# Two channel-major projections in seven products: the output gate and the gMLP gate of a hybrid trunk

## The chip, the cores and the metric

The kernel runs on one core of one Trainium2 chip. A core has five engines that each work through their own instructions in order: TensorE (PE, matrix products; PEld is its weight load), VectorE (DVE), ScalarE (ACT), GpSimd (POOL) and SyncE (SP, which issues the DMAs). The metric is the device time of one execution in microseconds; lower is better. Before the change it is 828.49 us, the median of 3 runs (826.92 to 829.87).

## The reference

One layer over 512 frames of 1024 channels, in float32. After an RMSNorm, one input projection of 7168 columns gives eight pieces: `zu, zv` (512 each), `zq, zf, zi, zo, g_a, g_b` (1024 each).

```
h = rmsnorm(x, norm_mix);  proj = h @ w_in
u = gelu(zu); v = layernorm(gelu(zv))
y_a = (u * (W_s v + b)) @ w_up_a            # gMLP: W_s mixes frames inside blocks of 128
f = sigmoid(zf), k = sigmoid(-zf), q = silu(zq), values = zi
o = recurrence(q, k, values, log f)          # HGRN2, 8 heads of 128
o = rmsnorm(o, norm_g) * silu(zo)            # the output gate
y_b = o @ w_up_b
mix = sigmoid(g_a) * y_a + sigmoid(g_b) * y_b
x = x + mix @ w_out
x = x + square(relu(rmsnorm(x) @ w_ff1)) @ w_ff2;  out = rmsnorm(x)
```

## The kernel before

**Arithmetic.** Each float32 operand is split into a high part H and a rest L (`split`, L95: H by ScalarE, L = x - H by VectorE), and a product is three matmuls, H times H, H times L, L times H (`mm3`, L113). Weights come as 512 KB tiles `raw` on SyncE's queue into 4 buffers (`wraw`, L89), in the order of `_plan`; their split (`operand`, L99) goes into 5 buffers `WH`/`WL`.

**Three forms of the input projection.** `chan_proj` (L314): 128 channels on the partitions, 512 frames wide, 8 blocks of k, so 24 matmuls of 512 columns. `tok_proj` (L332): frames on the partitions, 256 channels wide, 96 matmuls of 256 columns. `seven` (L124): 256 channels on the partitions by 512 frames as a 2x2 block product in seven block products instead of eight; each is 4 blocks of k in three matmuls, so 84 matmuls of 256 columns. It needs four sums of weight halves (`s1` to `s4`, L148 to L156) that are split as well, and frame operands `n1` to `n4` that are made once by `frames_operands` (L174). One product goes into an `acc` bank `x`, others into a pair of banks `zy`, of which there is one set in the first half of the kernel; `x` is read out in between.

**Order in the program around the change.** Normalised frames `hT`; `zv` by `tok_proj`; LayerNorm of `v` on VectorE and `frames_operands`; four groups of the gMLP branch, each with `chan_proj` for `zu` (L378), the block mixing `pm` and the product `y`; the values of round 0 (`values(0)`, L399); the upward projection `upa` into `part0`. Then four rounds of two heads. A round has `gates_round` (F and Q by `seven`), `hgrn_pair` (the recurrence: a chain of doublings on VectorE, small `sp` matmuls on TensorE, then `outputs` into `o_n` with frames on the partitions), the values of the next round and, from round 1 on, `gate_o` of the round before: `zo` by `tok_proj`, SiLU, product with `o_n`. Then gate A (four `seven`, L572), gate B (four `seven`, L576) with the last `gate_o` in the midst, and `onto_channels` (L583): eight heads of `o_n` are transposed (`py`), scaled by the norm's gain and split into `ybH`, `ybL`, which `upb` (L604) multiplies. The output projection and the MLP follow and are not touched.

**What sets the order.** The code's order is the priority; a scheduler then interleaves the instructions of each engine ahead of time, so that one `seven` is woven into another or into a round. On the chip each engine works in that fixed order and waits where an operand or a buffer is late. Tiles of a pool that is closed are handed on, tile by tile, once their last reader is done.

Of the kernel before, what the change touches and what calls it, by code (L numbers as in the profile page):

```python
# [48 lines left out]
def _plan():  # L49

    names = []
    for g in range(2):
        names += [("tok", ZV + 256 * g, k) for k in (0, 1)]
    names += [("chan", ZU + 128 * g) for g in range(4)]
    names += [("tok", ZI, k) for k in (0, 1)]
    names += [("upa", d) for d in range(4)]
    for r in range(4):
        names += [("tok", ZI + 256 * r, k) for k in (0, 1) if r]
        names += [("chan", z + 128 * h) for z in (ZF, ZQ) for h in (2 * r, 2 * r + 1)]
        names += [("tok", ZO + 256 * r, k) for k in (0, 1)]  # L60
    names += [("chan", GA + 128 * d) for d in range(8)]
# [12 lines left out]
def trunk_kernel(ctx: ExitStack, tc: tile.TileContext, A: dict, out: bass.AP):  # L74
# [156 lines left out]
    def rstd_of_halves(pool, ms, tag):  # L231

        e = pool.tile([P, 1], F32, tag=f"re_{tag}", bufs=2, name=f"re_{tag}")
        nc.gpsimd.tensor_scalar(e, ms[:, 0:1], EPS, None, ALU.add)
        return rstd_of(pool, ms[:, 1:2], 1, e, tag)
# [125 lines left out]
    px_stack.close()  # L361
    for t in range(NT):
# [13 lines left out]
    yaL = pya.tile([P, NG, S], F32R, name="yaL")  # L376
    for g in range(NG):
# [12 lines left out]
    def values(r):  # L390
        V = held("V", r).rearrange("p a b -> p (a b)").rearrange("p (t c) -> p t c", t=NT)

        def evac_v(tp, acc):
            nc.scalar.copy(V[:, 2 * tp:2 * tp + 2, :], acc)

        tok_proj(ZI + 256 * r, evac_v)
        return V

    V = values(0)  # L399


# [10 lines left out]
    left3 = ExitStack()  # L412
    pt = left3.enter_context(tc.tile_pool(name="pt", bufs=1, side="left", reuse_waits="tile"))
    left2 = ExitStack()
    hg = left2.enter_context(tc.tile_pool(name="hg", bufs=1, side="left", reuse_waits="tile"))
    ps_sc = left3.enter_context(tc.tile_pool(name="ps_sc", bufs=1, space=bass.MemoryType.PSUM))
# [10 lines left out]


    def gates_round(r, V):
# [6 lines left out]
        def fin_q(i, cols, src):  # L436
            qc = Q[:, i, cols]
            sig = pt.tile([P, S], F32, tag="sig", bufs=2, name="sig")[:, cols]
            nc.scalar.activation(sig, src, AF.Sigmoid, scale=-1.0 if i else 1.0)
            nc.vector.scalar_tensor_tensor(qc, src, -1.0 if i else 1.0, sig, ALU.mult, ALU.mult)  # L440
# [106 lines left out]
    def gate_a(d):  # L547
        g = pt.tile([P, 2, S], F32, tag="ga", bufs=1, name="ga")
# [47 lines left out]
    yb = [onto_channels(pyb, h) for h in range(4)]  # L596
    right2.close()
# [299 lines left out]
```

## Time and profile before

| what | value |
|---|---|
| median of the runs | 828.49 us |
| the profiled execution's own time | 830.5 us |
| its span, first to last instruction | 828.4 us |
| PE busy | 809.9 us, 98% |
| DVE busy | 597.6 us, 72% |
| ACT busy | 429.7 us, 52% |
| PE's clock, mean granted | 0.994 of full speed |

The busy time of an engine is the time in which at least one of its instructions is shown as running. Matmuls overlap: each is shown from its issue to the end of its result, so the time that one costs in a stream is the distance from its start to the next one's start, and not its shown duration. VectorE's instructions overlap a little at their ends in the same way.

### The profile page before, as it was taken

How to read it: one execution, taken by the hardware profiler on the slowest of the kernel's cores; microseconds unless marked ns; L12 is line 12 of the kernel's file. 1: busy time of each engine (PE TensorE's matmuls, PEld its weight loads, DVE VectorE, ACT ScalarE, POOL GpSimd, SP SyncE). 2: the span in 40 equal slices, each digit the busy share in tenths (PEclk: the TensorE clock that was granted, in tenths of full speed). 3: DMA queues.
4: the chain of work that ended last, by engine and by line, in shares of the span. 5: the costliest groups of instructions: out<-in, count | busy, mean ns of one | idle time of the engine just before them, and what ended most of it. 6: DMA issues, size and time to landing. Idle time of an engine off the chain costs nothing.

```text
span 828.4 us, 16602 instructions
## 1 busy us (share of the span) xinstructions
PE 809.9 (98%) x7026; PEld 740.8 (89%) x7026; DVE 597.6 (72%) x797; ACT 429.7 (52%) x720; POOL 49.4 (6%) x80
## 2 busy tenths in 40 slices
PE   8999999999999999999899999999999999999996
PEld 7989899998999999999778889999999988778884
DVE  6686257856767788865474369887777575899896
ACT  5543363637536446654432343767767542555464
POOL 2010000000000100100000022000000000010103
PEclk9999999999999999999999999999999999999998
DMA  8242232302313113332335411333333396193802
GB/s 315 73 143 64 63 105 79 104 28 81 99 53 103 52 54 102 102 103 81 123 102 168 162 56 48 97 109 102 103 104 118 117 296 176 40 283 93 239 10 102
DMA packets 27212, 92.29 MB, mean 111 GB/s; under 512 B 4161, under 2 KB 4161, under 8 KB 27138
## 3 DMA queue, kind: packets, MB, share of 16 engines
q1 hardware_dynamic: 24834, 83.89, 31.6%
q0 software_dynamic: 1728, 6.29, 4.2%
q8 instruction: 55, 0.90, 0.5%
q10 hardware_dynamic: 576, 1.05, 0.3%
q14 instruction: 19, 0.16, 0.1%
HBM read 89.13 MB, written 2.10 MB: 110 GB/s over the span
## 4 chain that ended last, share of the span: by engine, by line
PE 93%; ACT 2%; DVE 2%; DMA 1%; issue 1%; POOL 0%; SPq 0%; POOLq 0%; ACTq 0%; DVEq 0%
PE acc L120 12%; PE acc L121 11%; PE acc L122 11%; PE prodx L120 7%; PE prodx L121 7%; PE prodx L122 7%; PE prodzy L120 5%; PE prodzy L122 5%; PE prodzy L121 5%; PE hm L121 3%; PE hm L120 3%; PE hm L122 3%; PE sp L456 2%; PE y L122 2%; PE y L120 2%; PE y L121 2%
## 5 line engine op out<-in xcount | busy, mean ns | idle before, releaser
L97 DVE TENSOR_TENSOR WL<-raw,WH 128x1024 fp32r<-128x1024 f32 (+1 forms) x134 | 146.8, 1101 | 79.8 <-ACT WH L96 79.0
L96 ACT ACTIVATE WH<-raw 128x1024 fp32r<-128x1024 f32 (+1 forms) x134 | 128.7, 963 | 137.8 <-PE acc L121 27.2
L97 DVE TENSOR_TENSOR WL<-s,WH 128x1024 fp32r<-128x1024 f32 x60 | 73.3, 1222 | 39.7 <-ACT WH L96 38.9
L120 PE MATMUL acc<-WH,hTH 128*128 128x256 f32 x320 | 92.5, 289 | 1.3 <-ACT F L434 1.3
L121 PE MATMUL acc<-WL,hTH 128*128 128x256 f32 x320 | 91.4, 286 | 0.0
L122 PE MATMUL acc<-WH,hTL 128*128 128x256 f32 x320 | 91.0, 285 | 0.0
L96 ACT ACTIVATE WH<-s 128x1024 fp32r<-128x1024 f32 x60 | 63.7, 1062 | 39.0 <-PE prodx L121 15.7
L120 PEld LDWEIGHTS acc<-WH,hTH 128*128 128x128 f32 x320 | 60.9, 190 | 1.8 <-ACT F L434 1.6
L121 PEld LDWEIGHTS acc<-WL,hTH 128*128 128x128 f32 x320 | 61.0, 191 | 0.1
L122 PEld LDWEIGHTS acc<-WH,hTL 128*128 128x128 f32 x320 | 60.9, 190 | 0.0
L121 PE MATMUL hm<-WL,aH 128*128 128x512 f32 x96 | 38.1, 396 | 0.0
L122 PE MATMUL hm<-WH,aL 128*128 128x512 f32 x96 | 38.0, 395 | 0.0
L120 PE MATMUL hm<-WH,aH 128*128 128x512 f32 x96 | 37.9, 396 | 0.0
L120 PE MATMUL prodzy<-hTH,WH 128*128 128x256 f32 x128 | 36.2, 283 | 0.0
L122 PE MATMUL prodzy<-hTH,WL 128*128 128x256 f32 x128 | 36.0, 282 | 0.0
L121 PE MATMUL prodzy<-hTL,WH 128*128 128x256 f32 x128 | 36.0, 281 | 0.0
L120 PE MATMUL prodx<-n2H,WH 128*128 128x256 f32 x120 | 34.0, 283 | 0.7 <-ACT u L147 0.7
L96 ACT ACTIVATE WH<-rawx 128x1024 fp32r<-128x1024 f32 x24 | 25.1, 1054 | 18.5 <-issue 10.7
L120 PE MATMUL prodzy<-n1H,WH 128*128 128x256 f32 x120 | 33.8, 282 | 0.0
L120 PE MATMUL prodx<-n4H,WH 128*128 128x256 f32 x120 | 33.8, 282 | 0.0
L121 PE MATMUL prodx<-n4L,WH 128*128 128x256 f32 x120 | 33.8, 281 | 0.0
L122 PE MATMUL prodzy<-n1H,WL 128*128 128x256 f32 x120 | 33.6, 280 | 0.0
(313 smaller groups left out, 2494.3 us busy)
## 6 DMA issues: line engine op xcount, KB each, us to landing
raw<-in_w_dram SPq DMA_DIRECT2D x128, 512.0 KB, 3.7
rawx<-in_w_dram SPq DMA_DIRECT2D x18, 512.0 KB, 8.6
rawx<-in_w_dram POOLq DMA_DIRECT2D x6, 512.0 KB, 7.2
raw<-in_w_dram POOLq DMA_DIRECT2D x6, 512.0 KB, 8.5
part<-in_x_dram SPq DMA_DIRECT2D x4, 512.0 KB, 6.1
x<-in_x_dram SPq DMA_DIRECT2D x4, 512.0 KB, 6.5
out_dram<-x ACTq DMA_DIRECT2D x4, 256.0 KB, 2.7
out_dram<-x SPq DMA_DIRECT2D x4, 256.0 KB, 2.3
```

What stands on the lines that cost most here:

```text
L96: nc.scalar.activation(H, src, AF.Copy)
L97: nc.vector.tensor_tensor(L, src, H.bitcast(F32), ALU.subtract)
L120: nc.tensor.matmul(acc, ah, bh, start=first and i == 0, stop=False, **kw)
L121: nc.tensor.matmul(acc, ah, bl, start=False, stop=False, **kw)
L122: nc.tensor.matmul(acc, al, bh, start=False, stop=last and i == n - 1, **kw)
L456: nc.tensor.matmul(sp[p * C:(p + 1) * C, (h * NT + t) * n:(h * NT + t + 1) * n], K[:, h, c0:c0 + C], x(h, c0), start=True, stop=True)
```

## The change

The output gate `zo` is made with channels on the partitions by `seven` (four calls, one for two heads each), into tiles that earlier rounds held; SiLU is applied there. Its place is after the four rounds; gate A's four calls take the place in the rounds that `gate_o` had. `onto_channels` now multiplies the transposed, scaled head with the gate and splits the product, and its first four heads stand ahead of gate B in the code. `zu` is made by `seven` as well, in two calls. The values of rounds 0 and 1 are made before and after the gMLP groups. `rstd_of_halves` only gets other arguments.

```
-    names += [("tok", ZI, k) for k in (0, 1)]
+    names += [("tok", ZI + 256, k) for k in (0, 1)]
...
+    V = [values(0)]
     for g in range(NG):
-        zu = chan_proj(ZU + 128 * g)
-        u = gp.tile([P, S], F32, tag="u", bufs=2, name="u")
-        nc.scalar.activation(u, zu, AF.Gelu)
+        if g % 2 == 0:
+            u2 = pya.tile([P, 2, S], F32, tag="ug", bufs=1, name="ug")
+            seven(("chan", ZU + 128 * g), ("chan", ZU + 128 * g + 128), rhs, pya, ps_sc, u2, act_by_sign(u2, AF.Gelu), True)
+        u = u2[:, g % 2, :]
...
-    V = values(0)
+    V.append(values(1))
...
+    def silu(g, i, cols, src):
+        sig = hg.tile([P, S], F32, tag="sig", bufs=2, name="sig")[:, cols]
+        nc.scalar.activation(sig, src, AF.Sigmoid, scale=-1.0 if i else 1.0)
+        nc.vector.scalar_tensor_tensor(g[:, i, cols], src, -1.0 if i else 1.0, sig, ALU.mult, ALU.mult)
...
-    def gate_o(g):
-        def evac_zo(tp, acc):
-            sg = pt.tile([P, S], F32, tag="sig", bufs=2, name="sg").rearrange("p (j c) -> p j c", j=2)
-            nc.scalar.activation(sg, acc, AF.Sigmoid)
-            nc.vector.tensor_tensor(sg, acc, sg, ALU.mult)
-            ov = o_n[:, 2 * tp:2 * tp + 2, g * 256:(g + 1) * 256]
-            nc.vector.tensor_tensor(ov, ov, sg, ALU.mult)
-
-        tok_proj(ZO + 256 * g, evac_zo)
+    def gate_o(r, g):
+        seven(("chan", ZO + 256 * r), ("chan", ZO + 256 * r + 128), rhs, pt, ps_sc, g,
+              lambda i, cols, src: silu(g, i, cols, src), True)
+        return g
...
         hgrn_pair(r, *rounds[r])
         if r < 3:
-            rounds.append(gates_round(r + 1, values(r + 1)))
-        if r > 0:
-            gate_o(r - 1)
-    for d in range(0, KD, 2):
-        gate_a(d)
+            rounds.append(gates_round(r + 1, V[1] if r == 0 else values(r + 1)))
+        gate_a(2 * r)
+    sg = [gate_o(r, held(n, 4)) for r, n in enumerate("FQVK")]
     left2.close()
-    part1 = [held(n, 4) for n in "FQVK"]
-    for d in range(0, KD, 2):
-        merge_gate(GB, d, part1[d // 2])
-        if d == 2:
-            gate_o(3)
...
-        pyf = py.rearrange("p t v -> p (t v)")
-        nc.scalar.activation(H, pyf, AF.Copy, scale=hng)
-        nc.vector.scalar_tensor_tensor(L, pyf, hng, H.bitcast(F32), ALU.mult, ALU.subtract)
+        y = sg[h // 2][:, h % 2, :]
+        nc.vector.scalar_tensor_tensor(y, py.rearrange("p t v -> p (t v)"), hng, y, ALU.mult, ALU.mult)
+        split(y, H, L)
...
     yb = [onto_channels(pyb, h) for h in range(4)]
+    part1 = []
+    for r, n in enumerate("PVKP"):
+        part1.append(held(n, 5))
+        merge_gate(GB, 2 * r, part1[r])
```

First place, TensorE where the projection of `zu` begins. In the kernel before, the last products of `zv` are followed by 512-column products with `hTH`, `hTL` (the frames) as the moving side:

```order
L120 MATMUL acc<-WH,hTH 128x256
L121 MATMUL acc<-WL,hTH 128x256
L122 MATMUL acc<-WH,hTL 128x256
L120 MATMUL acc<-hTH,WH 128x512
L121 MATMUL acc<-hTL,WH 128x512
L122 MATMUL acc<-hTH,WL 128x512
```

In the changed kernel the values of round 0 come first, and the two calls for `zu` are woven into each other, with a mixing product `pm` between:

```order
L122 MATMUL prodzy<-n1L,WH 128x256
L123 MATMUL prodzy<-n1H,WL 128x256
L397 MATMUL pm<-wsT,v 128x128 x4
L121 MATMUL prodx<-hTH,WH 128x256
L122 MATMUL prodx<-hTL,WH 128x256
L121 MATMUL prodx<-n2H,WH 128x256
L122 MATMUL prodx<-n2L,WH 128x256
L123 MATMUL prodx<-n2H,WL 128x256
```

Each `zu` product is 256 columns wide now and needs frame operands (`n1`, `n2`) and weight sums from VectorE.

Second place, VectorE at the end of `frames_operands` (`n4L` is its last output). Before, the LayerNorm of `v` and the splits of plain weights follow:

```order
L97 TENSOR_TENSOR n4L<-o_n,n4H 128x1024
L368 TENSOR_SCALAR v<-v,mv,rr_l 128x512 x2
L97 TENSOR_TENSOR WL<-raw_816,WH 128x1024
L369 TENSOR_TENSOR v<-v,lng 128x512 x2
L370 TENSOR_TENSOR v<-v,lnb 128x512 x2
L97 TENSOR_TENSOR WL<-raw_850,WH 128x1024
```

In the changed kernel the sums (`s_793`, `s_794`) and splits of the second `zu` call (weights `raw_789`, `raw_791`) stand among them:

```order
L156 TENSOR_TENSOR s_794<-raw_789,raw_791 128x512
L98 TENSOR_TENSOR n4L<-o_n,n4H 128x1024
L98 TENSOR_TENSOR WL<-raw_646,WH 128x512
L150 TENSOR_TENSOR s_793<-s_793,raw_789 128x512
L371 TENSOR_SCALAR v<-v,mv,rr_l 128x512 x2
L98 TENSOR_TENSOR WL<-raw_789,WH 128x1024
L157 TENSOR_TENSOR s_794<-raw_789,s_793 128x512
L372 TENSOR_TENSOR v<-v,lng 128x512 x2
```

`WL<-raw_789` is the first operand of that second call, and the scaling of `v` by `rr_l` stands in front of it.

Third place, the passage from gate B's last `seven` to `upb`. Before, TensorE goes from the last product `n4` to `upb`, with the transposes `py` of the later heads between its matmuls:

```order
L122 MATMUL prodx<-n4H,WL 128x256
L120 MATMUL acc<-ybH_5169,WH 128x512 x2
L588 MATMUL py<-ident,o_n 128x128 x4
L121 MATMUL acc<-ybL_5170,WH 128x512
L122 MATMUL acc<-ybH_5169,WL 128x512
L120 MATMUL acc<-ybH_5178,WH 128x512
```

In the changed kernel no transpose is left there:

```order
L121 MATMUL prodx<-n4H,WH 128x256
L122 MATMUL prodx<-n4L,WH 128x256
L123 MATMUL prodx<-n4H,WL 128x256
L121 MATMUL acc<-ybH_4833,WH 128x512
L122 MATMUL acc<-ybL_4834,WH 128x512
L123 MATMUL acc<-ybH_4833,WL 128x512
```

ScalarE of the changed kernel at the same place; `P_5242<-prodx` is the read-out of that last product, and the splits `WH` are those of `upb`'s weights:

```order
L97 ACTIVATE WH<-raw_5521 128x1024
L172 ACTIVATE P_5242<-P_5242 128x256
L97 ACTIVATE WH<-raw_5556 128x1024
L172 ACTIVATE P_5242<-prodx 128x256
L97 ACTIVATE ybH_5370<-V_4571 128x512
L97 ACTIVATE ybH_5380<-V_4571 128x512
```

All eight transposes have moved in between gate products; of `ybH` the last four heads stand behind the read-out.

## Rows read from the trace of the kernel before

**Rows 1.** The page's head: span, busy time, and TensorE in 40 slices.

```profile
span 828.4 us, 16602 instructions
PE 809.9 (98%) x7026; PEld 740.8 (89%) x7026; DVE 597.6 (72%) x797; ACT 429.7 (52%) x720; POOL 49.4 (6%) x80
PE   8999999999999999999899999999999999999996
```

**Rows 2.** Groups by form: line, engine, operation, shapes, count | busy, mean ns | idle.

```profile
L120 PE MATMUL acc<-WH,hTH 128*128 128x256 f32 x320 | 92.5, 289 | 1.3 <-ACT F L434 1.3
...
L120 PE MATMUL prodx<-n4H,WH 128*128 128x256 f32 x120 | 33.8, 282 | 0.0
...
L120 PE MATMUL acc<-hTH,WH 128*128 128x512 f32 x32 | 12.8, 400 | 0.0
```

**Rows 3.** Timeline of TensorE, 39 to 46 us: start, duration, instruction.

```profile
39.08 0.28 PE L120 MATMUL acc<-WH,hTH 128*128 128x256 f32 x1
...
42.16 0.28 PE L122 MATMUL acc<-WH,hTL 128*128 128x256 f32 x1
42.28 0.39 PE L120 MATMUL acc<-hTH,WH 128*128 128x512 f32 x1
...
46.24 0.39 PE L122 MATMUL acc<-hTH,WL 128*128 128x512 f32 x1
```

**Rows 4.** Timeline of TensorE inside a `seven`, 304 to 308 us.

```profile
304.87 0.28 PE L120 MATMUL prodx<-n3H,WH 128*128 128x256 f32 x1
...
307.56 0.28 PE L122 MATMUL prodzy<-hTH,WL 128*128 128x256 f32 x1
```

**Rows 5.** Timeline of VectorE in a gate A `seven`, 340 to 347 us.

```profile
340.12 0.42 DVE L160 TENSOR_TENSOR ga<-prodx,u 128x256 f32<-128x256 f32 x1
340.45 0.68 DVE L148 TENSOR_TENSOR s<-raw 128x512 f32<-128x512 f32 x1
...
345.15 0.68 DVE L156 TENSOR_TENSOR s<-raw,s 128x512 f32<-128x512 f32 x1
345.75 1.22 DVE L97 TENSOR_TENSOR WL<-raw,WH 128x1024 fp32r<-128x1024 f32 x1
346.88 1.22 DVE L551 TENSOR_TENSOR part<-part,ga 128x1024 f32<-128x1024 f32 x1
```

**Rows 6.** Busy time in three stretches: window, then each engine's us.

```profile
110.00:400.00 290.00, 285.32 (x3874) 276.95 (x3873) 211.82 (x335) 154.91 (x332) 12.99 (x16) 1.00 0.29 85
260.00:320.00 60.00, 60.00 (x882) 58.50 (x881) 47.38 (x79) 28.59 (x66) 3.48 (x4) 1.00 0.26 79
720.00:780.00 60.00, 60.00 (x258) 48.21 (x257) 59.11 (x59) 32.21 (x32) 5.22 (x6) 1.00 0.73 209
```

**Rows 7.** Timeline of VectorE, 31 to 55 us; in brackets its idle time and releaser.

```profile
31.63 1.29 DVE L364 BATCH_NORM_STATS2 bn<-v 128x6 f32<-128x512 f32 x2 [1.15 <-ACT v L359]
...
33.98 0.55 DVE L368 TENSOR_SCALAR v<-v,mv,rr_l 128x512 f32<-128x512 f32 x1 [0.32 <-POOL rr_l L228]
...
54.52 1.17 DVE L368 TENSOR_SCALAR v<-v,mv,rr_l 128x512 f32<-128x512 f32 x2 [1.05 <-POOL rr_l L228]
```

**Rows 8.** Timeline of TensorE from gate B's end into `upb`.

```profile
396.39 0.28 PE L122 MATMUL prodx<-n4H,WL 128*128 128x256 f32 x1
399.12 1.18 PE L120 MATMUL acc<-ybH,WH 128*128 128x512 f32 x2 [2.44 <-ACT ybH L590]
...
414.97 0.50 PE L120 MATMUL acc<-ybH,WH 128*128 128x512 f32 x1 [0.33 <-DVE F L609]
```

**Rows 9.** Timeline of ScalarE at the same place.

```profile
396.64 1.06 ACT L96 ACTIVATE WH<-raw 128x1024 fp32r<-128x1024 f32 x1 [0.34 <-PE prodx L121]
397.60 0.37 ACT L171 ACTIVATE K<-prodx 128x256 f32<-128x256 f32 x1
397.87 0.62 ACT L171 ACTIVATE K<-K 128x512 f32<-128x512 f32 x1
398.39 1.26 ACT L590 ACTIVATE ybH<-py,hng 128x512 fp32r<-128x512 f32 x2
```

**Rows 10.** Timeline of TensorE: a transposed head between gate products.

```profile
354.75 0.28 PE L122 MATMUL prodx<-hTH,WL 128*128 128x256 f32 x1
354.87 0.60 PE L588 MATMUL py<-ident,o_n 128*128 128x128 f32 x4
355.22 0.37 PE L120 MATMUL prodzy<-n1H,WH 128*128 128x256 f32 x1
355.43 0.28 PE L121 MATMUL prodzy<-n1L,WH 128*128 128x256 f32 x1
```

More of the change, by code (lines that the diff above doesn't have):

```diff
@@ L53, in _plan @@
         names += [("tok", ZV + 256 * g, k) for k in (0, 1)]
+    names += [("tok", ZI, k) for k in (0, 1)]
     names += [("chan", ZU + 128 * g) for g in range(4)]
-    names += [("tok", ZI, k) for k in (0, 1)]
+    names += [("tok", ZI + 256, k) for k in (0, 1)]
     names += [("upa", d) for d in range(4)]
     for r in range(4):
-        names += [("tok", ZI + 256 * r, k) for k in (0, 1) if r]
+        names += [("tok", ZI + 256 * r, k) for k in (0, 1) if r > 1]
         names += [("chan", z + 128 * h) for z in (ZF, ZQ) for h in (2 * r, 2 * r + 1)]
-        names += [("tok", ZO + 256 * r, k) for k in (0, 1)]
-    names += [("chan", GA + 128 * d) for d in range(8)]
+        names += [("chan", GA + 128 * (2 * r + i)) for i in range(2)]
+    names += [("chan", ZO + 128 * h) for h in range(8)]
     names += [("chan", GB + 128 * d) for d in range(8)]
@@ L229, in rstd_of, with rstd_of_halves @@
         return r2
-    def rstd_of_halves(pool, ms, tag):
+    def rstd_of_halves(pool, early, late, tag):
         e = pool.tile([P, 1], F32, tag=f"re_{tag}", bufs=2, name=f"re_{tag}")
-        nc.gpsimd.tensor_scalar(e, ms[:, 0:1], EPS, None, ALU.add)
-        return rstd_of(pool, ms[:, 1:2], 1, e, tag)
+        nc.gpsimd.tensor_scalar(e, early, EPS, None, ALU.add)
+        return rstd_of(pool, late, 1, e, tag)
     def mean_square(junk, x, ms):
@@ L361, in trunk_kernel @@
     px_stack.close()
+    ps_stack = ExitStack()
+    ps_sc = ps_stack.enter_context(tc.tile_pool(name="ps_sc", bufs=1, space=bass.MemoryType.PSUM))
     for t in range(NT):
@@ L376, in trunk_kernel, with values, evac_v @@
     yaL = pya.tile([P, NG, S], F32R, name="yaL")
+    def values(r):
+        V = held("V", r).rearrange("p a b -> p (a b)").rearrange("p (t c) -> p t c", t=NT)
+        def evac_v(tp, acc):
+            nc.scalar.copy(V[:, 2 * tp:2 * tp + 2, :], acc)
+        tok_proj(ZI + 256 * r, evac_v)
+        return V
+    V = [values(0)]
     for g in range(NG):
-        zu = chan_proj(ZU + 128 * g)
-        u = gp.tile([P, S], F32, tag="u", bufs=2, name="u")
-        nc.scalar.activation(u, zu, AF.Gelu)
+        if g % 2 == 0:
+            u2 = pya.tile([P, 2, S], F32, tag="ug", bufs=1, name="ug")
+            seven(("chan", ZU + 128 * g), ("chan", ZU + 128 * g + 128), rhs, pya, ps_sc, u2, act_by_sign(u2, AF.Gelu), True)
+        u = u2[:, g % 2, :]
         pm = ps.tile([P, NT, P], F32, tag="hm", bufs=2, name="pm")
@@ L388, in trunk_kernel @@
         split(y, yaH[:, g, :], yaL[:, g, :])
[L390 to L397, printed above, removed]
-    V = values(0)
+    V.append(values(1))
     for d in range(KD):
@@ L411, in trunk_kernel @@
     hv = left.enter_context(tc.tile_pool(name="hv", bufs=1, side="left", reuse_waits="tile"))
-    left3 = ExitStack()
-    pt = left3.enter_context(tc.tile_pool(name="pt", bufs=1, side="left", reuse_waits="tile"))
+    pt = left.enter_context(tc.tile_pool(name="pt", bufs=1, side="left", reuse_waits="tile"))
     left2 = ExitStack()
     hg = left2.enter_context(tc.tile_pool(name="hg", bufs=1, side="left", reuse_waits="tile"))
-    ps_sc = left3.enter_context(tc.tile_pool(name="ps_sc", bufs=1, space=bass.MemoryType.PSUM))
     nc.sync.dma_start(hng, A["hg_norm_g"].rearrange("o v -> v o"))
@@ L436, in fin_q @@
         def fin_q(i, cols, src):
[L437 to L440, printed above, removed]
+            silu(Q, i, cols, src)
         for z, g, fin in ((ZF, F, fin_f), (ZQ, Q, fin_q)):
@@ L547, in gate_a @@
     def gate_a(d):
-        g = pt.tile([P, 2, S], F32, tag="ga", bufs=1, name="ga")
+        g = hg.tile([P, 2, S], F32, tag="ga", bufs=1, name="ga")
         merge_gate(GA, d, g)
@@ L551, in gate_a @@
         nc.vector.tensor_tensor(ua, ua, g, ALU.mult)
-    def gate_o(g):
-        def evac_zo(tp, acc):
-            sg = pt.tile([P, S], F32, tag="sig", bufs=2, name="sg").rearrange("p (j c) -> p j c", j=2)
-            nc.scalar.activation(sg, acc, AF.Sigmoid)
-            nc.vector.tensor_tensor(sg, acc, sg, ALU.mult)
-            ov = o_n[:, 2 * tp:2 * tp + 2, g * 256:(g + 1) * 256]
-            nc.vector.tensor_tensor(ov, ov, sg, ALU.mult)
-        tok_proj(ZO + 256 * g, evac_zo)
-    rounds = [gates_round(0, V)]
+    def gate_o(r, g):
+        seven(("chan", ZO + 256 * r), ("chan", ZO + 256 * r + 128), rhs, pt, ps_sc, g,
+              lambda i, cols, src: silu(g, i, cols, src), True)
+        return g
+    rounds = [gates_round(0, V[0])]
     for r in range(4):
@@ L596, in trunk_kernel @@
     yb = [onto_channels(pyb, h) for h in range(4)]
+    part1 = []
+    for r, n in enumerate("PVKP"):
+        part1.append(held(n, 5))
+        merge_gate(GB, 2 * r, part1[r])
+    ps_stack.close()
     right2.close()
```

5 lines of the change are left out of this document (2 added, 3 removed).

## The prediction

> **What bounds the kernel now.** I read the page's head first: TensorE is busy for 809.9 of 828.4 us, and no slice between the first and the last is below eight tenths [rows 1]. So the time is TensorE's stream, plus 18.5 us of its gaps, and a change is worth what it takes out of that stream. The next view to read is the timeline and not the grouped table: the table shows 282 to 289 ns for a matmul of 256 columns and 400 ns for one of 512 [rows 2], but those spans overlap. In the timeline, the 27 matmuls of a token projection from 39.08 to 42.16 start 0.1185 us apart, the 18 matmuls of 512 columns from 42.28 to 46.24 start 0.233 us apart [rows 3], and the 24 of a `seven` from 304.87 to 307.56 start 0.117 us apart [rows 4]. These distances price the change. Last comes VectorE by stretches: 211.8 of 290 us (73%) in the rounds and gates, 47.4 of 60 in the busiest round, and 59.1 of 60 in the closing products, in both of the latter with TensorE busy throughout [rows 6].
>
> **The output gate.** `gate_o` as token projection is 4 x 96 = 384 matmuls, 45.5 us at 0.1185. As `seven` it is 4 x 84 = 336, 39.3 us at 0.117. All of it lies on the path: -6.2 us.
>
> **The gMLP gate.** Four `chan_proj` are 96 matmuls of 512 columns, 22.4 us at 0.233. Two `seven` are 168 of 256 columns, 19.7 us at 0.117: -2.7 us.
>
> **What VectorE gets for it.** Back to back it takes 1.13 us for 1024 elements, 0.60 for 512 and 0.33 for 256 (distances of starts) [rows 5]. One `seven` is three splits of 1024, a split of 512, four sums and one addition of 512, one addition of 256: 3.39 + 3.60 + 0.33 = 7.3 us. Two for `zu` less four old splits of 1024: +10.1. Four for `zo` (29.3) and their SiLU products (4 x 1.26), less eight splits of 1024 and sixteen products of 512: +15.7. `onto_channels` has two operations of 512 per head instead of one: +4.8. Together 30.6 us more. I cost them at nothing where TensorE's work covers them, and check that for the two crowded places.
>
> *Rounds and gates.* Into the stretch of 290 us come the 15.7 us, eight scalings of heads and four of their splits (7.2; most of this work lay behind the stretch), and two splits of moved values leave (2.3): 211.8 + 20.6 = 232.4 us. TensorE's stretch is shorter by 6.2 and by the 96 matmuls of the values that are made earlier (11.3): 272.5 us. VectorE would be 85% busy. Its cover is what the closing stage shows, 98% with TensorE never idle [rows 6]; so I take 0. The other end, the 79% of the busiest round, is a rival below. Below zero the limit is the 4.7 us that TensorE idles in this stretch now.
>
> *The start of `zu`.* VectorE is at its limit from 31.63 us on; its only gaps until 54.52 are 0.32 and 1.05 us of waiting for `rr_l` from GpSimd [rows 7]. In the changed order, from the `BN_STATS` at 31.63 to `WL<-raw_789`, the first operand of the second `zu` call, I count 13 operations of 1024 elements (14.7), 13 of 512 (7.8), four scalings of `v` at 0.5 and two small ones: 24.7 to 25.0 us, so it is ready at about 56.5. TensorE gets there after the moved values (42.28 + 96 x 0.1185 = 53.7), 24 product matmuls (2.8) and four mixing ones, whose price I take from four transposes, 0.35 us plus the restart of 0.1 [rows 10]: 56.9. They meet within half a microsecond. The waits for `rr_l` stand in front of that operand on VectorE and would be passed on to TensorE, which takes its work in order: between 0 and 1.4 us; I take 0.9. Behind it the later operands have several microseconds of slack.
>
> **The passage to `upb`.** TensorE now ends gate B at 396.39 and starts `upb` at 399.12, since `ybH` comes behind ScalarE's last split and two gate read-outs; 0.33 us more is lost at 414.97 [rows 8, 9]. The distance of starts less one matmul is 2.6 us, so 2.9 in all. Afterwards no transpose is left there, the first four heads are ready, but `upb`'s second accumulator needs the bank of the last product. Its read-out `P_5242<-prodx` stands on ScalarE behind the split `WH<-raw_5556`, which itself needs a buffer that this last product frees. Queued behind it are the last four `ybH`, which TensorE wants twelve 512-column matmuls later. So 0.96 for the split, 0.37 for the read-out [rows 9], a handover of 0.1, and the 0.33 again: 1.7. Net -1.2 us. Bounds: -2.9 if the split gets its buffer early, 0 if the last heads are late as well. The transposes themselves cost the same in either place, 0.35 us for four [rows 10], and there are eight groups before and after.
>
> **Nothing** for the rest: as many 512 KB loads in as many buffers, and the same operations on GpSimd. ScalarE gains some splits and read-outs, but is busy for 52% [rows 1] and has 155 of 290 us in the stretch [rows 6].
>
> **The sum.** -6.2 - 2.7 + 0.9 - 1.2 = -9.2 us. Against the profiled execution's own 830.5 us that is 821.3. That execution lies 2.0 us above the median of the runs, 828.5, and the forecast is for the median: 819.3 us.
>
> **Rivals.**
>
> *VectorE takes over in the rounds and gates (slower).* The recurrence's doublings, the SiLU products and the heads' scalings stand in one fixed queue with the weight splits that TensorE waits for, and a bank pair `zy` comes free only after a VectorE addition. For it: in the stretch as it is, VectorE never had to be above 79% over 60 us [rows 6]. Against it: 98% in the closing stage, although there is no recurrence there. If it can't be packed above 79%, 232.4 / 0.79 = 294 us in place of 272.5: 819.3 + 21.7 = 841 us. The change is lost below 232.4 / 281.7 = 82.5%.
>
> *The start of `zu` stalls (no change).* All of the 10.1 us that VectorE gets there come on the path, in place of the 0.9: 828.5 us. For it: VectorE has no slack there [rows 7]. Against it: the moved values give 11.3 us of cover.
>
> *The narrow product costs more than half of the wide one (no change).* The shown durations have the ratio 0.282 to 0.400 [rows 2]. If that ratio held for the distances, 256 columns would cost 0.164 where 512 cost 0.233, `zu` would be 27.6 us in place of 22.4, +5.2 where I have -2.7: 827.2 us. Rows 3 and 4 speak against it, since 0.117 is half of 0.233. The Trainium skill's page "TensorE: Matmul & The Clock Gate", section "Back-to-back issue gap", has such a rule: in a stream of weight loads and matmuls it gives about 81 ns for 128 columns and 131 ns for 512. By a straight line between its two figures 256 columns would be an estimated 98 ns, and `zu` would lose 3.9 us. The trace disagrees with both the level and the ratio, and the measurement decides.
>
> **How the numbers follow.** The forecast has 0.72, with a range of its own from 814.6 (the 4.7 us of idle time vanish) to 824; the stall of `zu` 0.15, VectorE's takeover 0.10, the price of narrow products 0.03. A measurement of this kernel tells about 0.3%, 2.5 us, from no change, so faster is below 826.0 and slower above 831.0. The forecast and the milder half of the stall (0.06) give 0.78 for faster; the rest of the stall, the narrow products and a small part of the takeover 0.13 for the same; the remainder of the takeover 0.09 for slower. From 814.5 to 827.5 lies the forecast, and most of the stall's outcomes; the takeover is left out.
>
> **What would show it.** Right: matmuls of `zo` and `zu` 0.117 us apart; TensorE busy near 801 us and its idle time not above 20; VectorE busy about 630 us; a gap of about 1.5 us ahead of `upb`, released by ScalarE. Wrong: in the gates, TensorE's gaps released by VectorE's `WL` or by the additions of `zy`, with VectorE above 95% or TensorE's idle time there above 10 us; a gap of several microseconds at the first products of the second `zu` call; starts farther apart than 0.12 us.

## The result and the profile after

The changed kernel takes 820.01 us (median of 4 runs, 818.54 to 820.87) against 829.18 us before (4 runs, 826.92 to 831.0): ratio 0.9889, 95% interval 0.9858 to 0.992. In a later comparison it took 820.22 against 828.12 us (6 and 11 runs), ratio 0.9901 [0.9881, 0.9921]. So it is faster by 8 to 9 us, and the forecast of 819.3 us lies within 1 us of both medians. Its profiled execution took 818.54 us.

The page's head after, the answer to [rows 1]:

```profile
span 816.6 us, 16756 instructions
PE 799.0 (98%) x7050; PEld 734.4 (90%) x7050; DVE 626.5 (77%) x849; ACT 445.7 (55%) x756; POOL 53.4 (7%) x80
PE   8999999999999999999999999999999999999996
```

TensorE is busy for 10.9 us less, its idle time went from 18.5 to 17.6 us, and VectorE is busy for 28.9 us more. That was forecast: TensorE near 801, VectorE about 630, idle not above 20.

Timeline of TensorE where the two `zu` calls are woven into each other, to be read against [rows 3, 4]: nine distances from 55.48 to 56.53, 0.117 us each, without a gap. The last line is the first matmul that needs `WL` of the second call's plain weights.

```profile
55.48 0.28 PE L123 MATMUL prodx<-n2H,WL 128*128 128x256 f32 x1
...
56.53 0.28 PE L123 MATMUL prodx<-n2H,WL 128*128 128x256 f32 x1
...
59.45 0.28 PE L123 MATMUL prodx<-hTH,WL 128*128 128x256 f32 x1
```

Timeline of VectorE there, the answer to [rows 7]. The wait for `rr_l` still stands in front of the split of that operand, but TensorE runs on.

```profile
29.02 1.29 DVE L367 BATCH_NORM_STATS2 bn<-v 128x6 f32<-128x512 f32 x2 [0.56 <-ACT v L360]
...
53.67 1.16 DVE L371 TENSOR_SCALAR v<-v,mv,rr_l 128x512 f32<-128x512 f32 x2 [1.06 <-POOL rr_l L229]
54.75 1.22 DVE L98 TENSOR_TENSOR WL<-raw,WH 128x1024 fp32r<-128x1024 f32 x1
```

Timeline of TensorE at the passage, the answer to [rows 8]:

```profile
394.29 0.28 PE L123 MATMUL prodx<-n4H,WL 128*128 128x256 f32 x1
395.92 0.50 PE L121 MATMUL acc<-ybH,WH 128*128 128x512 f32 x1 [1.35 <-ACT P L172]
...
404.71 0.50 PE L121 MATMUL acc<-ybH,WH 128*128 128x512 f32 x1 [0.33 <-DVE P L608]
```

And of ScalarE, the answer to [rows 9]: the split, then the read-out that TensorE waits for.

```profile
394.54 1.06 ACT L97 ACTIVATE WH<-raw 128x1024 fp32r<-128x1024 f32 x1 [0.97 <-ACT P L172]
395.50 0.37 ACT L172 ACTIVATE P<-prodx 128x256 f32<-128x256 f32 x1
```

Every landmark that the prediction named is there. The terms, however, did not all have the right size, and two profiles differ by more than the change does; both are worked out below.

### The profile page after: what moved, and what is told of

Its sections match the earlier page's. It is cut to its first block, busy times and chain, and to the rows that moved or that the text cites. A ratio compares the mean times of both kernels' runs of the same rounds, so it can differ in the third digit from the quotient of the medians.

```text
span 816.6 us, 16756 instructions
## 1 busy us (share of the span) xinstructions
PE 799.0 (98%) x7050; PEld 734.4 (90%) x7050; DVE 626.5 (77%) x849; ACT 445.7 (55%) x756; POOL 53.4 (7%) x80
## 4 chain that ended last, share of the span: by engine, by line
PE 44%; DVE 3%; issue 1%; ACT 1%; POOL 1%; POOLq 0%; ACTq 0%; DVEq 0%
PE acc L121 5%; PE acc L122 5%; PE acc L123 5%; PE prodx L121 3%; PE prodx L122 3%; PE prodx L123 3%; PE hm L121 3%; PE hm L122 2%; PE hm L123 2%; PE prodzy L121 2%; PE prodzy L123 2%; PE prodzy L122 2%; PE y L121 2%; PE y L123 2%; PE y L122 2%; DVE WL L98 1%
## 5 line engine op out<-in xcount | busy, mean ns | idle before, releaser
L98 DVE TENSOR_TENSOR WL<-s,WH 128x1024 fp32r<-128x1024 f32 x72 | 87.8, 1221 | 26.4 <-ACT WH L97 25.6
L121 PE MATMUL acc<-WH,hTH 128*128 128x256 f32 x192 | 54.7, 286 | 0.1
L123 PE MATMUL acc<-WH,hTL 128*128 128x256 f32 x192 | 54.4, 284 | 0.0
L122 PE MATMUL acc<-WL,hTH 128*128 128x256 f32 x192 | 54.1, 283 | 0.0
L121 PE MATMUL prodzy<-hTH,WH 128*128 128x256 f32 x176 | 50.4, 286 | 1.3 <-ACT u L153 1.3
L123 PE MATMUL prodzy<-hTH,WL 128*128 128x256 f32 x176 | 49.8, 283 | 0.0
L123 PE MATMUL prodx<-n4H,WL 128*128 128x256 f32 x144 | 40.3, 280 | 0.0
L122 PE MATMUL prodx<-n2L,WH 128*128 128x256 f32 x144 | 40.2, 279 | 0.0
L122 PE MATMUL prodzy<-n1L,WH 128*128 128x256 f32 x144 | 40.2, 279 | 0.0
L123 PE MATMUL prodx<-n2H,WL 128*128 128x256 f32 x144 | 40.2, 279 | 0.0
```

The source lines that it names most:

```text
L98: nc.vector.tensor_tensor(L, src, H.bitcast(F32), ALU.subtract)
L121: nc.tensor.matmul(acc, ah, bh, start=first and i == 0, stop=False, **kw)
L122: nc.tensor.matmul(acc, ah, bl, start=False, stop=False, **kw)
L123: nc.tensor.matmul(acc, al, bh, start=False, stop=last and i == n - 1, **kw)
```

## Where the time went, by stretches

The rounds and gates, to be read beside [rows 6], from the last matmul of `upa` to the last `n4` of gate B, and the pieces at the passage. Busy time by stretch of the kernel before (window, length, then PE, PEld, DVE, ACT, POOL, then PE's granted clock):

```profile
103.20:396.40 293.20, 290.96 (x3926) 282.88 (x3924) 210.79 (x333) 155.84 (x332) 14.20 (x18) 1.00 0.28 84
...
398.00:400.00 2.00, 0.88 (x2) 0.56 (x3) 1.88 (x3) 1.64 (x3) 0.00 (x0) 0.80 0.76 238
400.00:402.00 2.00, 2.00 (x8) 1.80 (x8) 0.60 (x2) 0.69 (x1) 0.00 (x0) 0.50 0.99 277
402.00:404.00 2.00, 2.00 (x11) 1.62 (x10) 0.66 (x1) 0.26 (x1) 0.00 (x0) 0.85 0.49 199
```

The same of the changed kernel; from 392 to 412 its clock is 1.00 in every window of 2 us:

```profile
109.80:394.30 284.50, 280.95 (x3818) 271.01 (x3816) 231.53 (x372) 165.88 (x357) 15.34 (x18) 1.00 0.28 85
```

*The passage.* Before, behind the gap of 2.44 us, the granted clock was 0.50 (1.2 GHz of 2.4) for a while, and TensorE's 512-column matmuls stood 0.43 us apart instead of 0.233. Timeline of TensorE before:

```profile
401.38 0.63 PE L122 MATMUL acc<-ybH,WL 128*128 128x512 f32 x1
401.81 0.63 PE L120 MATMUL acc<-ybH,WH 128*128 128x512 f32 x1
```

From the last `n4` to the last `upb` matmul it is 51.13 us before and 42.99 after. Of the 8.1 us, 12 `upb` matmuls (2.8) and six transposed heads (2.6) only moved ahead of the last `n4`; 2.7 us are a true gain. The gap itself gave 1.1, as forecast; the other 1.6 is the clock: the three windows above, granted 0.80, 0.50 and 0.85, lack (0.20 + 0.50 + 0.15) x 2 = 1.7 us of full clock. The stretch before is 51.40 and 51.41 us in the two experiments that keep the old passage, and 42.96 to 43.00 in five others that keep the new one.

*The rounds.* 293.20 - 11.4 (96 matmuls of moved values) - 6.2 (`zo`) + 2.8 + 2.6 (moved in) = 281.0 us were to be expected; there are 284.5, so 3.5 us were lost. TensorE's idle time there went from 2.2 us (293.20 - 290.96) to 3.5 (284.50 - 280.95), for instance by this wait (timeline of TensorE after):

```profile
189.19 0.38 PE L121 MATMUL prodzy<-hTH,WH 128*128 128x256 f32 x1 [1.32 <-ACT u L153]
```

The other 2.2 us show as busy time: 280.95 us, where 290.96 - 12.2 = 278.8 was to be expected. They are not broken down further.

*The start.* To the first matmul of `upa` it is 79.6 us before and 86.3 after, with 11.4 us of values moved in: a gain of 4.7, where `zu` was to give 1.8 net. The 168 `zu` matmuls take 19.96 us (distances of starts added up) and the 96 wide ones 22.72, so `zu` gave 2.8. Another 2.3 us come from the first 20 us of the execution, which the change doesn't touch. Timeline of TensorE before:

```profile
14.32 0.41 PE L120 MATMUL acc<-WH,hTH 128*128 128x256 f32 x1
14.54 0.41 PE L121 MATMUL acc<-WL,hTH 128*128 128x256 f32 x1
...
19.09 1.05 PE L301 MATMUL pt<-dr,xg 128*128 128x128 f32 x8
```

And after:

```profile
13.16 0.28 PE L121 MATMUL acc<-WH,hTH 128*128 128x256 f32 x1
13.28 0.28 PE L122 MATMUL acc<-WL,hTH 128*128 128x256 f32 x1
...
16.77 1.05 PE L302 MATMUL pt<-dr,xg 128*128 128x128 f32 x8
```

In the first microseconds 256-column matmuls start 0.213 us apart, later 0.117, and when that turns differs between executions: the fourth row of transposes `pt` starts at 16.53 to 18.54 us in six profiles of kernels that are the same up to there (the changed one twice, and the four with a lengthened gap below), and at 16.99 in a kernel that is like the one before up to 42 us. It is chance and no effect of the change. It is the clock: 0.213 us is the distance that 256-column matmuls have where the clock is granted at 0.50, and the trace's own record of the granted clock begins with 1.00 at 16.9 us in the kernel before, at 12.3 in the changed one and at 15.6 in the one with eight extra reads below, whose distances turn at 15.64. (Ahead of the record's first entry the row of the profile shows 1.00 for want of an entry.) The Trainium skill's page "TensorE: Matmul & The Clock Gate", section "Part 1: The HAM clock gate (the "warmup" mystery)", says that the array is throttled by default, and that the point of the turn differs by ±500 ns between executions. The trace agrees with the low rate at the start and shows a wider spread: in the six profiles the record begins between 11.2 and 15.6 us, and the work behind it moves by 2.0 us.

*Behind `upb`.* From the last `upb` matmul to the end it is 380.9 us before and 379.3 after, 1.6 us less. The change does reach this part: the other arguments of `rstd_of_halves` take one of three GpSimd operations out of the chain that the last normalisation waits for. Timeline of GpSimd before:

```profile
821.92 0.56 POOL L234 TENSOR_SCALAR re_f<-ms 128x1 f32<-128x1 f32 x1 [1.07 <-ACT junk L239]
...
822.93 0.57 POOL L228 TENSOR_TENSOR rr_f<-rs_f,neghalf 128x1 f32<-128x1 f32 x1
```

And after:

```profile
810.46 0.63 POOL L227 TENSOR_SCALAR rs_f<-ms,re_f 128x1 f32<-128x1 f32 x1 [0.83 <-ACT junk L240]
811.17 0.57 POOL L229 TENSOR_TENSOR rr_f<-rs_f,neghalf 128x1 f32<-128x1 f32 x1
```

That gives 0.3 us. From the start of the last matmul to the end it is 8.47 to 8.49 us in the three profiles with the old arguments and 8.10 to 8.13 in the eleven with the new ones. The other 1.3 us are no more than executions of one program differ there: in the six profiles named above the part takes 379.3 to 381.2 us.

## The experiments

The theory at first was the prediction's own: `zo` 6.2, `zu` 2.7, the passage, and the early values as cover for the start of `zu`. Its rivals were another price for narrow products, a VectorE without room, and a scheduler that fills the start in any order.

**The `zu` part alone** (the kernel before with the change's hunks on `zu` and on `values`):

```
-        zu = chan_proj(ZU + 128 * g)
+        if g % 2 == 0:
+            u2 = pya.tile([P, 2, S], F32, tag="ug", bufs=1, name="ug")
+            seven(("chan", ZU + 128 * g), ...)
...
+    V = [values(0)]            # ahead of the groups
+    V.append(values(1))        # behind them
```

> The kernel before with the gMLP gate alone by seven products, and the values of rounds 0 and 1 moved as in the change; the output gate stays a token projection. Theory (the time is TensorE's stream): 96 matmuls of 512 columns at 0.233 us become 168 of 256 at 0.117, -2.7 us, less 0 to 1.4 us where the second call waits for VectorE; 1.3 to 2.7 us below the kernel before, and the 2.6 us gap ahead of upb stays. Rival (a narrow product costs more than half of a wide one): +5 us. Rival (VectorE stalls the start of zu): no change or slower, with a gap of several us near 55 us.

832.11 us (12 runs) against 828.58 (24 runs): ratio 1.0035 [1.0016, 1.0054], slower: neither the 1.3 to 2.7 us of gain nor a gap near 55 us, which the rival had. In the profile the start gains 4.3 us (79.6 + 11.4 - 86.7), of which 2.0 are the chance of the first 20 us. Then the recurrence of the first round stalls; timeline of TensorE, and busy time by stretch:

```profile
181.71 0.49 PE L539 MATMUL po<-V,scores 128*128 128x128 f32 x2 [1.15 <-DVE st L533]
183.97 0.79 PE L539 MATMUL po<-V,scores 128*128 128x128 f32 x2 [1.77 <-ACT hjunk L543]
```

```profile
110.20:398.70 288.50, 283.82 (x3830) 274.73 (x3828) 208.80 (x331) 152.28 (x328) 14.13 (x18) 0.98 0.28 82
...
184.00:186.00 2.00, 2.00 (x49) 1.74 (x49) 0.33 (x2) 0.37 (x2) 0.00 (x0) 0.50 0.00 0
...
192.00:194.00 2.00, 2.00 (x70) 1.96 (x70) 0.60 (x1) 1.63 (x4) 0.00 (x0) 0.51 0.03 8
```

The rounds take 288.5 us where 293.2 - 11.4 = 281.8 would be right: 6.7 us lost, more than `zu` gives, and that with no more work for VectorE there (208.80 us against 210.79). Some 3 us are idle time at the recurrence: before, matmuls of values stand among it until 181 us, here the last of them starts at 168. Then the clock is granted at 0.50 from 184 to 194 us, which costs up to 5 us. Not every execution had it: the two of twelve with a mean granted clock of 0.996 and 0.998 took 828.60 and 829.24 us, like the kernel before, and the other ten, at 0.988 to 0.991, took 830.38 to 834.80. So a gain of `zu` doesn't stand alone: what its hunk takes out of the rounds counts as well.

**The `zo` part alone** (the changed kernel with `chan_proj` for `zu` again; the early values stay):

```
...
-            seven(("chan", ZU + 128 * g), ("chan", ZU + 128 * g + 128), rhs, pya, ps_sc, u2, act_by_sign(u2, AF.Gelu), True)
-        u = u2[:, g % 2, :]
+        zu = chan_proj(ZU + 128 * g)
...
+        nc.scalar.activation(u, zu, AF.Gelu)
```

> The changed kernel with zu back in its four plain channel projections; output gate by seven products, gate A in the rounds, transposes beside gate B. Theory: 384 matmuls become 336, -6.2 us, and the passage to upb -1.2 us: 7.4 us below the kernel before, 1.8 to 2.7 above the changed kernel. Rival (the gain comes from the moves and not from the products): more than 8 us below the kernel before, or TensorE's busy time not lower by 6.

824.16 us (7 runs), ratio 0.9946 [0.9925, 0.9966] to the kernel before: 4.4 us below the kernel before, where 7.4 were expected, and TensorE is busy for 4.4 us less (805.5) instead of 6, which is what the rival asked for. What is missing is again the loss in the rounds: they last 284.6 us, as in the changed kernel. So `zo`'s 6.2 us are not disproved here, but not shown either; the next run shows them. The kernel is 4 us above the changed one, for which `zu` gives 2.8. The rest goes with the clock: the two of seven executions with a mean granted clock of 0.998 took 822.33 us, the other five, at 0.995 and 0.996, took 824.12 to 825.71. In the profile the first part falls out as slowly as before (the fourth `pt` row at 19.05 us), and the clock falls to 0.50 near 518 us, behind two waits that the changed kernel has as well.

**The values at their old places** (the changed kernel otherwise):

```
-    V = [values(0)]            # ahead of the groups
...
-    V.append(values(1))
+    V = [values(0)]
...
-            rounds.append(gates_round(r + 1, V[1] if r == 0 else values(r + 1)))
+            rounds.append(gates_round(r + 1, values(r + 1)))
```

> The changed kernel with the values of rounds 0 and 1 where they were before: zu's first call starts right after zv, 11 us earlier. Theory (the moved values are the cover of VectorE's work for zu): TensorE reaches the second call's first operand some 9 us before VectorE has it; TensorE idles 6 to 10 us between 44 and 60 us, and the time is 6 to 10 us above the changed kernel's. Rival (VectorE's work there is covered anyway, by the planned order): within 2 us of the changed kernel.

820.8 us (6 runs), ratio 0.9903 [0.9884, 0.9922]: no difference from the changed kernel. The theory, that without the early values the time rises by 6 to 10 us, fell. Busy time by stretch of this kernel, the rounds and then the start of `zu`:

```profile
103.60:394.90 291.30, 290.53 (x3914) 281.84 (x3912) 233.95 (x374) 169.70 (x361) 15.93 (x18) 1.00 0.29 87
42.00:80.00 38.00, 34.76 (x286) 33.53 (x285) 34.52 (x49) 18.99 (x29) 3.64 (x4) 1.00 0.40 111
```

Without them TensorE idles 3.2 us at the start of `zu`, against 0.1 from 42 to 86 us in the changed kernel; so much was the theory's cover worth there. In return it idles 0.8 us in the rounds (291.30 - 290.53) against 3.5. The 96 matmuls cover waits wherever they stand, and are worth as much in one place as in the other: the rounds take 291.3 - 11.4 = 279.9 without them, 4.6 us less than the changed kernel's 284.5. This run also shows that `zo` is worth its full 6.2 us, and that VectorE's additional work in the rounds costs nothing while the values stand there: TensorE's busy time goes from 290.96 to 290.53, 0.4 us less, where -6.2 + 2.8 + 2.6 = -0.8 was worked out.

**Narrow products alone** (the kernel before, each 512-column product of `chan_proj` as two of 256):

```
-        mm3(acc, [(blk(W, k), (hTH[:, k, :], hTL[:, k, :])) for k in range(KD)])
+        for hs in (slice(0, 256), slice(256, S)):
+            mm3(acc[:, hs], [(blk(W, k), (hTH[:, k, hs], hTL[:, k, hs])) for k in range(KD)])
```

> The kernel before, in which each plain channel projection of zu is done as two halves of 256 frames: 192 matmuls of 256 columns in place of 96 of 512, the same multiplications and weights. Theory (a column costs the same in both widths): 22.5 us in place of 22.4, no change. Rival (256 columns cost 0.164 us where 512 cost 0.233): +9 us.

828.19 us (12 runs), ratio 0.9989 [0.9975, 1.0003]. 192 narrow products cost what 96 wide ones did; the rival that gave the narrow one more than half is excluded.

**The changed kernel again, and without its gap at the passage** (the last gate B call puts its `prodx` into another bank, so that `upb`'s second accumulator doesn't wait for the read-out):

```
-        xtag = "acc" if tight else "hm"
+        xtag = xtag or ("acc" if tight else "hm")
...
-        merge_gate(GB, 2 * r, part1[r])
+        merge_gate(GB, 2 * r, part1[r], "hm" if r == 3 else None)
```

> The changed kernel once more, beside the others on the same chip: 820 us, 9 below the kernel before.

> The changed kernel, in which the last gate B call has its x product in a bank of the other tag, so that upb's second accumulator need not wait for its read-out behind a weight split on ScalarE. Theory: the 1.5 us gap ahead of upb goes, 1 to 1.5 us below the changed kernel in the trace, if the last heads' transposes, which use the same tag, are not late in its place. Rival: the last four heads (ScalarE's and VectorE's splits behind that point) are what ends the wait; the gap stays or moves by a few matmuls, no change.

820.22 us (6 runs) for the first and 818.75 us (4 runs, 818.22 to 819.48) for the second, ratio to before 0.988 [0.9862, 0.9898]. The two intervals overlap. In the trace the gap of 1.35 us is gone, but a wait of 0.44 us for the last heads' `ybL` has come in its place, as the rival had it in part, and the passage takes 42.14 us instead of 42.98. So 0.8 of the 1.5 us between the medians is shown. Timeline of TensorE of the second:

```profile
394.42 0.28 PE L123 MATMUL prodx<-n4H,WL 128*128 128x256 f32 x1
...
394.89 0.48 PE L123 MATMUL acc<-ybH,WL 128*128 128x512 f32 x1
...
398.32 0.50 PE L122 MATMUL acc<-ybL,WH 128*128 128x512 f32 x1 [0.44 <-DVE ybL L98]
```

It has the lowest median of all kernels here, and confirms that the wait of 1.35 us was for the bank, as the prediction had it.

**More work for VectorE** (three, then six statistics of 512 elements more in each of 20 `seven` calls, whose results nobody uses):

```
+        if tight and pool is not pya:
+            for i in range(3):
+                nc.vector.bn_stats(extra, hTH[:, 0, :].bitcast(F32))
...
+    extra = cst.tile([P, 6], F32, name="extra")
```

> The changed kernel with three VectorE statistics of 512 elements more in each of the 20 calls of the rounds and gates, on data that nobody waits for (results unused): 20 x 3 x 0.60 = 36 us of VectorE. Its busy time in the rounds and gates goes from 231 to 267 of 292 us, 91%. Theory (VectorE still has room there): within 3 us of the changed kernel. Rival (VectorE can't be packed above 82% beside the recurrence): 267 / 0.82 = 326 us, 34 us above it.

> As the last one with six statistics per call: 72 us of VectorE, 303 us of work in a stretch of 292. Theory: VectorE is now the bound there; at least 11 us above the changed kernel, 17 us if it packs to 98%, and TensorE's gaps are released by VectorE. Rival (packing at 82%): 303 / 0.82 = 370, 77 us above it.

839.19 us (4 runs), ratio 1.0127 [1.0109, 1.0145], and 842.18 us (4 runs), ratio 1.0168 [1.0146, 1.019]: 19 and 22 us more than the changed kernel. The theory that there is room for it fell with the smaller dose, and the share of VectorE doesn't explain it either. Stretch of the rounds with three operations per call, and the timeline of TensorE:

```profile
111.60:410.20 298.60, 290.08 (x3818) 280.32 (x3816) 245.59 (x395) 165.99 (x357) 15.07 (x18) 0.98 0.27 81
```

```profile
18.45 0.28 PE L123 MATMUL acc<-WH,hTL 128*128 128x256 f32 x1
...
20.97 0.28 PE L121 MATMUL acc<-WH,hTH 128*128 128x256 f32 x1
...
148.17 0.39 PE L121 MATMUL prodx<-n4H,WH 128*128 128x256 f32 x1 [0.90 <-DVE F L164]
153.96 0.39 PE L123 MATMUL prodx<-hTH,WL 128*128 128x256 f32 x1 [1.55 <-DVE WL L98]
...
197.24 0.49 PE L545 MATMUL po<-V,scores 128*128 128x128 f32 x2 [1.15 <-DVE st L539]
198.82 0.49 PE L545 MATMUL po<-V,scores 128*128 128x128 f32 x2 [1.10 <-ACT hjunk L549]
```

And the stretch with six:

```profile
111.20:412.00 300.80, 290.41 (x3818) 279.17 (x3816) 277.38 (x454) 165.47 (x356) 15.20 (x18) 0.98 0.27 79
```

VectorE is 82% busy with the smaller dose and 92% with the larger, and the stretch grows by 14 and 16 us. With the same 3818 matmuls TensorE's idle time is 8.5 and 10.4 us instead of 3.5, and its busy time 9 us longer.

Not all of this is VectorE's doing, for the edit changed more than its work. From 18.45 to 20.97 us, before the first of the added operations (27.7 us), 21 distances of matmuls of 256 columns are 0.120 us each, where the changed kernel has 0.117, and so it goes on through the rounds in both of these kernels. The stretch has 1872 matmuls of this width (20 calls of 84, two projections of 96); at 0.003 us each that is an estimated 5.6 us. None of the other twelve profiles has it. Behind `upb`, where none of the added operations stands, the kernel with three takes 384.7 us and the changed one 380.3, part of it by a fall of the clock near 531 us. What widens the distances is not shown; the edit also adds a small constant tile. So at most 8.5 of the 14 us are due to VectorE's work: 5.0 of more idle time, and for the rest mostly the low clock (0.98 over the stretch).

Of the idle time 2.9 us stand from 145 to 154 us, in the gates of the first round, most of it released by VectorE's additions and splits, as the prediction's rival has it; 2.8 us stand from 196 to 200 us at `po`, where the `zu` part alone has its stall; 1.9 us stand at 211 us in the recurrence that follows. A second flaw of the test: since the operations depend on nothing late, the scheduler put 31 of the 60 between 42 and 111 us, 23 from there to 200 us and the rest earlier still, so it shows what a lag in the first round costs, and gives no share of VectorE at which the rounds would stop.

**A longer gap at the passage.** After this the theory was that a cluster of gaps is followed by a low clock and so costs twice. ScalarE reads the last product two, four or eight times more before its proper read-out; the order of TensorE's work ahead of the gap stays the same:

```
+            if i == 1 and cols.start == 0:
+                for j in range(late):
+                    nc.scalar.copy(g[:, i, cols], src)
             fin(i, cols, src)
```

> The changed kernel, in which ScalarE reads gate B's last product twice more before its proper read-out, so that TensorE's gap ahead of upb grows by 2 x 0.27 = 0.5 us, from 1.5 to about 2.0 (extra reads, same output). Theory (a gap costs its length, and a second time when the granted clock falls behind it): +0.5 if the clock stays at 1.00, up to +2.2 if it falls as it did behind the gap of 2.6 us in the kernel before. Rival (a gap costs its length alone, the fall of the clock in the kernel before had another cause): +0.5 and a clock of 1.00 behind the gap.

> As the run with two extra reads, with four: the gap ahead of upb grows by 1.1 us to about 2.6, the size that it had in the kernel before. Theory: the granted clock falls to 0.50 behind the gap for two to four us, and the stretch from the last n4 to the end of upb grows by 1.1 + 1.7 = 2.8 us. Rival: the clock stays at 1.00 and the stretch grows by 1.1 us.

> With eight extra reads: the gap ahead of upb grows by 2.2 us to about 3.7. Theory: the granted clock falls to 0.50 behind the gap, the stretch from the last n4 to the end of upb grows by 2.2 + 1.7 = 3.9 us or more (up to 2.2 + 5 if the low clock lasts as long as behind the stall of round 1 in the kernel with the zu part alone). Rival: +2.2 us and a clock of 1.00.

> The kernel with four extra reads once more. The profile with two extra reads had the same gaps ahead of upb (1.87 and 0.58 us) as the one with four (1.87 and 0.57), but the clock stayed at 1.00 there and fell to 0.50 here. Theory (whether the clock falls behind gaps of this size is settled anew in each execution): this profile can show 1.00 and a stretch of 43.7 us from the last n4 to the end of upb, like the one with two reads. Rival (the program's own order behind the gap settles it): the clock falls again and the stretch is 46.6 us.

| extra reads | median us | ratio to before | gaps at the passage | lowest clock behind | last `n4` to end of `upb` |
|---|---|---|---|---|---|
| none | 820.22 | 0.9901 [0.9881, 0.9921] | 1.35, 0.33 | 1.00 | 42.98 |
| two | 821.11 | 0.9911 [0.9891, 0.993] | 1.87, 0.58 | 1.00 | 43.74 |
| four | 822.04 | 0.9918 [0.9894, 0.9943] | 1.87, 0.57 | 0.50 | 46.57 |
| four again | 820.99 | 0.9913 [0.9881, 0.9945] | 1.87, 0.57 | 0.50 | 45.32 |
| eight | 824.86 | 0.9956 [0.9935, 0.9977] | 1.87, 0.57, 0.78 | 1.00 | 44.80 |

Timeline of TensorE with two extra reads:

```profile
397.12 0.49 PE L121 MATMUL acc<-ybH,WH 128*128 128x512 f32 x1 [1.87 <-ACT ybH L97]
398.19 0.50 PE L122 MATMUL acc<-ybL,WH 128*128 128x512 f32 x1 [0.58 <-DVE ybL L98]
```

With four, and the clock in its stretches:

```profile
396.83 0.50 PE L121 MATMUL acc<-ybH,WH 128*128 128x512 f32 x1 [1.87 <-ACT ybH L97]
397.90 0.80 PE L122 MATMUL acc<-ybL,WH 128*128 128x512 f32 x1 [0.57 <-DVE ybL L98]
398.50 0.63 PE L123 MATMUL acc<-ybH,WL 128*128 128x512 f32 x1
398.92 0.63 PE L121 MATMUL acc<-ybH,WH 128*128 128x512 f32 x1
```

```profile
398.00:400.00 2.00, 2.00 (x5) 1.61 (x6) 1.66 (x3) 1.73 (x5) 0.00 (x0) 0.50 0.62 209
...
402.00:404.00 2.00, 2.00 (x6) 1.56 (x5) 0.96 (x2) 1.06 (x1) 0.00 (x0) 0.50 0.00 0
```

Neither theory holds as it stood. The gaps with two and four extra reads are equal within 0.01 us, and behind the one the clock stayed at 1.00 and behind the other it was 0.50 for 6 us. With eight, 3.2 us of gaps left it at 1.00; its run is 3.6 us above the unlengthened one's profile, 1.8 of it here and 1.2 by the chance of the first 20 us. In the two executions with four reads the gaps are equal, and the low clock cost 2.8 and 1.6 us beyond the 43.74. So a fall can follow such gaps and then costs 1.6 to 2.8 us, but it need not, and its length changes from execution to execution. The same kernel's time follows it: with four reads the four runs had mean clocks of 0.990, 0.993, 0.995 and 0.997, and times of 824.41, 822.93, 820.79 and 821.14 us.

The same shows at a place that no edit here touches. Ahead of the first `seven` of the MLP, two waits of TensorE of 0.83 to 0.87 and 0.73 to 0.74 us stand in all fourteen profiles. Timeline of TensorE there in the `zo` part alone:

```profile
516.29 0.38 PE L121 MATMUL prodx<-h2H,WH 128*128 128x256 f32 x1 [0.86 <-ACT WH L97]
```

And in the changed kernel:

```profile
511.43 0.39 PE L121 MATMUL prodx<-h2H,WH 128*128 128x256 f32 x1 [0.86 <-ACT WH L97]
```

Behind them the clock was granted at 0.50 for some 3 us in seven profiles (the `zo` part alone, the late values, the narrow products, both with more work for VectorE, one of the two with four reads, and the one with eight) and at 1.00 in the other seven, the kernel before and both profiles of the changed one among them. What settles whether the clock falls stays open.

## Why the prediction was right, step by step

| step | predicted | in the runs |
|---|---|---|
| `zo` by `seven` | -6.2 | -6.2, by the run with late values to within 0.4 |
| `zu` by `seven` | -2.7 | -2.8 |
| start of `zu` | +0.9 | +0.4 (2.8 + 2.3 - 4.7), no wait |
| VectorE's 30.6 us and the moved values | 0 | +3.5 in the rounds |
| passage to `upb` | -1.2 | -2.7 |
| last normalisation | 0 | -0.3 |
| sum | -9.2 | -8.1; medians -9.2 and -7.9 |

The two profiled spans differ by more, 11.8 us: the 8.1, the 2.3 of chance at the start and 1.3 behind `upb`. That the first median came within 0.1 us of the forecast's 9.2 is luck, since the terms add up to 8.1 and the second median has 7.9.

The price of the products was right, since it was taken from distances of starts. At the start of `zu` the count of VectorE's work was right, and the path was not. From `BN_STATS` to the end of the split it is 27.0 us (29.02 to 55.97), of which 1.6 are waits (0.56 and 1.06) and 25.3 work; 24.7 to 25.0 were counted. But the prediction has TensorE need that operand as soon as it begins the second call, at 54.93 us here. In the order on the chip only two matmuls with the high part `WH` stand there, 36 of the first call follow, and the first one with `WL` starts at 59.45 us, 3.5 us after the split. So no wait for `rr_l` was passed on, and the 0.4 us are no wait for VectorE: TensorE idles 0.1 us there, and the 96 moved matmuls, with restarts between them, take 11.75 us (distances of starts added up) instead of 11.4.

Two terms were mis-sized, by +3.5 and -1.5 us, and their errors cancel in part. The first is the step "I take 0" in the rounds. It subtracted the 11.3 us of moved values as if nothing else hung on them. The run with late values shows that they were cover for the rounds: there TensorE waits for 0.8 us with VectorE at 234 us of work, with the values gone 3.5. VectorE's own load, on which the step argued (85% against the closing stage's 98%), was not what decided: the `zu` part alone lost 6.7 us there with VectorE at 208.8 us of work, less than before, and 92% was reached with the larger dose. The second is the passage. The gap shrank from 2.77 to 1.68 us, as worked out, but the slow clock behind the old gap, visible in the rows of before above, had not been read; it was worth another 1.6 us. All three profiles with the old passage show it. A third term was put at nothing, "the same operations on GpSimd": one of them left the chain at the end, 0.3 us.

Of the rivals, the stall of `zu` and the price of narrow products didn't come. VectorE's takeover didn't come either, but it was nearer than its chance said: 14 us more of VectorE's work in the rounds (245.6 - 231.5) cost up to 8.5 us there. In part that came in the rival's way, by gates that wait for VectorE's additions and splits; in part by the recurrence of one round that is left without cover, with the slow clock on top. A share of busy time at which it sets in was not found.

## What to carry to other kernels

A block of independent matmuls that is moved is taken out of one place as cover and put into another: both places are to be priced, and if both were tight, moving it is worth nothing. Read the granted clock behind every gap of a microsecond or more, since the stretch behind it can hold as much as the gap. And before two profiles are subtracted, compare a stretch that the change can't touch: here it alone differed by 2.3 us, a quarter of the effect. The same goes for an edit that is meant to add work alone: with it the distances of matmuls went from 0.117 to 0.120 us even ahead of the first added operation, an estimated 5.6 of the 14 us that it seemed to cost in the rounds.

## What was not expected of the hardware

The granted clock fell to 0.50 behind idle time of TensorE of 1.6 to 2.9 us, in one or two pieces: 2.4 us in the kernel before (at 399 us), 2.9 with the `zu` part alone (184), 1.9 with four extra reads (397), 1.6 in the `zo` part alone (518). It stayed there for 3 to 10 us, in which matmuls of 512 columns stood 0.43 us apart and those of 256 columns 0.213; behind equal or longer idle stretches in other executions it stayed at 1.00. In the first 10 to 17 us of an execution matmuls stand just as far apart, and the trace's record of a clock of 1.00 begins only where that ends. And in the two kernels with more work for VectorE matmuls of 256 columns stood 0.120 us apart through the rounds, at a granted clock of 1.00, where all others have 0.117; why is not shown.
